# Emitting three RWKV quads ahead of the windowed attention, and spreading the residual's spill over weight chunks

## The chip, the cores and the metric

The kernel runs on one core of one Trainium2 chip. The metric is the device time of one execution in microseconds (us). TensorE (PE) does matrix products into PSUM, VectorE (DVE) and ScalarE (ACT) do element-wise work, GpSimd (POOL) a few memory fills, and SyncE (SP) starts nearly all transfers (DMA). Each engine runs its own instructions strictly in the order in which they stand in the program and waits on semaphores for the others.

## The reference

A sequence of 256 tokens of width 2048 passes through two blocks. The first (S5 and DeltaNet branches, then a gated feed-forward net) and the context path of the second are not touched. In the second block, cut to what matters here:

```python
x = rmsnorm(first_block(x), final_norm_w)                 # the residual of the second block
z = modulate(rmsnorm(x), sh1, sc1) @ w_in
q, k, v = axial_rope(...)                                 # 16 query heads, 4 key/value heads of 64
attn = windowed_gqa(q, k, v, kc, vc, sink)                # softmax over a band and 256 context tokens
r, v, kk, dirs, gate = rwkv_prepare(z)                    # 16 heads of 64, two directions
for d in range(2):                                        # S = S*w + (S.-kk) b^T + v k^T ; y = S r
    y += wkv_scan(S_ctx[d], r, w[d], k[d], v, kk, a[d], reverse=d == 1)
rw = (groupnorm(y) + bonus) * gate
x = x + g1 * (concat(attn, rw) @ w_out)
x = x + g2 * swiglu(modulate(rmsnorm(x), sh2, sc2))
return rmsnorm(x, final_norm_g)
```

## The kernel before

Activations lie feature-major (features on the 128 partitions, 256 tokens along the free axis). Every large product goes through `dense`: a weight chunk of 256 by up to 512 elements is loaded, ACT rounds it (`wr`, L269), DVE takes the remainder (`wl`, L270), and PE does three products of 256 columns for each 128x128 block (L298, L299, L301), 24 for a full chunk. The chunk has three load buffers and two for each half.

The RWKV recurrence is done by `rw_quad`, four heads at a time, in chunks of 64 tokens. A quad has a front (`rw_front`: gates, decays, the operands BK and AR, then chunk products that become the masked N and M, L1355), the inverse of a triangular matrix in 16x16 blocks on DVE (L571 to L607), a merge of the blocks to 64x64 in which PE, DVE and ACT take turns (L627 to L655), and four chunk steps, each of which needs the state S left by the one before: px (PE, L1433), X (DVE, L1436), pa (PE, L1445), two copies into SAV (ACT L1447, DVE L1448), pS (PE, L1452), two updates of S (DVE, L1458 and L1459). `rw_quad` is a generator, and `early` draws from several so that a quad's front is emitted before the one ahead of it ends.

`attention` runs over 4 key/value heads, 2 query blocks and 2 pairs of heads: 16 units. A unit is at_ps (PE, L1667 and L1670), two row maxima (DVE, L1674), their scaling (L1676, once a unit), two exponentials (ACT, L1680), transposes (PE, L1683), copies (L1685) and at_po (PE, L1689). After two units the sums are inverted and the result is scaled (L1706). `attn_split`, `x3_load` (the residual read back from memory) and `w_out2(0)`, the output projection of the attention's half in 384 products, follow; then the gate (`rw_out_gate`, L1547 to L1549), the group norm `rw_out` for the four quads (L1565 to L1578, with the root at L416, the reciprocal at L417 and the spread at L425), and `w_out2(1)`.

`x2_spill` scales the residual by the norm of the first block's end in 16 DVE instructions (L1174) and writes it out in four transfers. It is called between the projection of the first keys and `rw_lora`.

Each engine's order is made by a scheduler that takes, of what is ready in its own model of time, the instruction that was emitted first. So the order of calls in `program` is an order of priority, and work that is emitted later fills the places where earlier work can't run. All of it is fixed before the run.

Of the kernel before, what the change touches and what calls it, by code (L numbers as in the profile page):

```python
# [14 lines left out]
ALU = mybir.AluOpType  # L15
# [74 lines left out]
class Kern:  # L90
# [182 lines left out]
    def dense(self, W, KT, c0, w, xh, xl, evac, r0=0):  # L273
# [7 lines left out]
        for k0 in range(0, KT, 2):  # L281
# [7 lines left out]
            for b, part in order:  # L289
                for j in range(b * per, min(b * per + per, nft)):  # L290
                    m = min(128, w - j * 128)
                    o = banks[b][:m, j % per]
                    first_j, last_j = j % per == 0, j % per == per - 1 or j == nft - 1
                    for k in range(kb):
                        kt = k0 + k
                        a = (wr, wl)[part][:, k, j * 128:j * 128 + m]
                        if part == 0:
                            nc.tensor.matmul(o, lhsT=a, rhs=xh(kt), start=kt == 0 and first_j, stop=False)  # L298
                            nc.tensor.matmul(o, lhsT=a, rhs=xl(kt), start=False, stop=False)  # L299
                        else:  # L300
                            nc.tensor.matmul(o, lhsT=a, rhs=xh(kt), start=False, stop=kt == KT - 1 and last_j)  # L301
            self.ticks += self.tick_rate
            while self.ticks >= 1:
                self.ticks -= 1
# [2 lines left out]
        for i, b in enumerate(banks):  # L307
            evac(i, b)


    ticks = 0.0
    tick_rate = 0.72
# [851 lines left out]
    def x2_spill(self):  # L1164
        nc = self.nc
        x = self.x1
        fw = self.P("final_norm_w")
        r = self.rsqrt(self.s1, 1.0 / (32 * D), self.eps["e6"])
        self.x2d = self.pd.tile([D, T], F32, name="x2d")
        xd = self.x2d.rearrange("(k p) t -> p k t", p=128)  # L1170
        for i, t in enumerate(x.tiles):
            for k in range(4):
                kt = i * 4 + k
                nc.vector.scalar_tensor_tensor(x(kt), x(kt), fw[:, kt:kt + 1], r, ALU.mult, ALU.mult)  # L1174
            nc.sync.dma_start(xd[:, i * 4:i * 4 + 4], t)

    def mod1(self):

# [342 lines left out]
    def rw_x(self, half):  # L1521
        h = (self.hh, self.hl)
        if half == 0:

            self.rwR = {"kkn": [None, None]}
            self.rw_cols(self.rwR, h, "k", "x", 0)
            self.x2_spill()
            self.rw_lora(self.rwR, h, "x")
        self.rw_cols(self.rwR, h, "kvr"[1 - half:], "x", half)
        if half:  # L1530
# [254 lines left out]
    def program(self, out):  # L1785
# [28 lines left out]
        self.rw_x(1)  # L1814
        self.attn_cols()
        self.ada_end()
        self.attention()
        self.early([self.rw_xq(1, ()), self.rw_xq(2, ('AR',)), self.rw_xq(3, ('AR',))])
        self.attn_split()
        self.x3_load()  # L1820
        self.w_out2(0)
# [112 lines left out]
```

## Time and profile before

| what | value |
|---|---|
| median of 3 runs | 3485.99 us (3480.36 to 3486.3) |
| the profiled execution | 3484.27 us, its span 3482.5 us |
| PE busy | 3341.5 us (96%), 30680 instructions |
| DVE busy | 2506.8 us (72%), 4245 instructions |
| ACT busy | 1515.8 us (44%), 2148 instructions |
| granted TensorE clock | 0.975 of 2.4 GHz over the span |

The profiled execution lies 1.7 us under the median, so sums are made against 3484.27 us. Times in the trace are counted from the span's start. In the rows below a busy PE is not PE at its peak: products are pipelined, and at the lower clock level each takes longer and still counts as busy. Of the order's rows, fp32 products appear twice in the trace's counts.

### The profile page before, as it was taken

The numbers are of one execution on the slowest core, as the hardware profiler recorded it, in microseconds if no ns is written. First come the engines' busy times: TensorE is split into PE (matmuls) and PEld (weight loads), VectorE is DVE, ScalarE is ACT, GpSimd is POOL, SyncE is SP. The second block draws the span as 40 slices with busy tenths as digits, with TensorE's granted clock in tenths as the row PEclk, the third lists the DMA queues.
The fourth block names the chain that finished last, engine by engine and source line by source line (L and its number), as shares of the span: only waits on it lengthen the run. The fifth ranks groups of instructions, "written<-read, shape, count | busy, mean of one in ns | idle before, by whom it ended". The sixth has DMA issues, their size and how long they took to land. (4 is left out here: it accounts for less than half of the span.)

```text
span 3482.5 us, 72752 instructions
## 1 busy us (share of the span) xinstructions
PE 3341.5 (96%) x30680; PEld 3073.5 (88%) x30680; DVE 2506.8 (72%) x4245; ACT 1515.8 (44%) x2148; POOL 17.0 (0%) x46
## 2 busy tenths in 40 slices
PE   8999999999999999999999999998898999999998
PEld 7889767898998889999999988886686999999997
DVE  7787777877668878967777778686666666665556
ACT  5434334444454444434444454443433443333433
POOL 0000000000000000000000000000000000000000
PEclk9999999999998999999999999997899999999999
DMA  7655555667654445456676664450123676655554
GB/s 234 184 167 172 179 173 183 190 217 254 209 176 158 139 160 165 157 192 225 227 230 219 223 198 148 141 174 2 33 98 100 211 226 225 228 188 182 182 187 146
DMA packets 337287, 618.37 MB, mean 178 GB/s; under 512 B 25184, under 2 KB 49504, under 8 KB 336960
## 3 DMA queue, kind: packets, MB, share of 16 engines
q1 hardware_dynamic: 336736, 612.66, 54.7%
q8 instruction: 240, 3.93, 0.5%
q0 software_dynamic: 224, 1.07, 0.1%
q14 instruction: 87, 0.71, 0.1%
HBM read 608.39 MB, written 4.72 MB: 176 GB/s over the span
## 5 line engine op out<-in xcount | busy, mean ns | idle before, releaser
L270 DVE TENSOR_TENSOR wl<-w,wr 128x1024 fp32r<-128x1024 f32 (+2 forms) x928 | 1110.5, 1197 | 654.2 <-ACT wr L269 619.8
L269 ACT CAST wr<-w 128x1024 fp32r<-128x1024 f32 (+2 forms) x928 | 953.3, 1028 | 1382.6 <-PE acc L299 1172.0
L298 PE MATMUL acc<-hh,wr 128*128 128x256 f32 (+2 forms) x4976 | 1255.1, 287 | 35.0 <-DVE conv L378 10.3
L299 PE MATMUL acc<-hl,wr 128*128 128x256 f32 (+2 forms) x4976 | 1247.8, 286 | 5.1 <-DVE hl L317 3.2
L298 PEld LDWEIGHTS acc<-hh,wr 128*128 128x128 f32 (+2 forms) x4976 | 957.7, 193 | 75.5 <-issue 31.3
L299 PEld LDWEIGHTS acc<-hl,wr 128*128 128x128 f32 (+2 forms) x4976 | 958.6, 193 | 22.7 <-issue 16.4
L301 PE MATMUL acc<-hh,wl 128*128 128x256 f32 (+2 forms) x4976 | 749.6, 286 | 6.5 <-DVE wl L270 6.4
L301 PEld LDWEIGHTS acc<-hh,wl 128*128 128x128 f32 (+2 forms) x4976 | 660.5, 193 | 30.9 <-DVE wl L270 10.9
L298 PE MATMUL acc<-hid,wr 128*128 128x256 f32 x1408 | 355.6, 286 | 3.1 <-DVE x L1128 3.0
L299 PE MATMUL acc<-hid,wr 128*128 128x256 f32 x1408 | 353.3, 284 | 0.0
L298 PEld LDWEIGHTS acc<-hid,wr 128*128 128x128 f32 x1408 | 270.2, 192 | 7.2 <-DVE x L1128 3.7
L299 PEld LDWEIGHTS acc<-hid,wr 128*128 128x128 f32 x1408 | 270.3, 192 | 1.5 <-issue 1.1
L242 DVE SCALAR_TENSOR_TENSOR w_ada<-w_ada,ada_c 128x512 f32<-128x512 f32 x384 | 260.2, 679 | 3.8 <-PE ada_c L235 3.3
L301 PE MATMUL acc<-hid,wl 128*128 128x256 f32 x1408 | 223.9, 285 | 1.5 <-DVE wl L270 1.5
L301 PEld LDWEIGHTS acc<-hid,wl 128*128 128x128 f32 x1408 | 191.9, 192 | 4.4 <-DVE wl L270 1.9
L1107 DVE SCALAR_TENSOR_TENSOR fconv<-acc,pv,fconv 128x255 f32<-128x255 f32 (+1 forms) x176 | 81.2, 477 | 16.5 <-ACT fconv L1105 14.7
L298 PE MATMUL acc<-mrgh,wr 128*128 128x256 f32 x256 | 65.1, 289 | 2.9 <-ACT wr L269 2.9
L299 PE MATMUL acc<-ys5l,wr 128*128 128x256 f32 x256 | 64.3, 287 | 2.3 <-DVE ys5l L317 2.3
L298 PE MATMUL acc<-ys5h,wr 128*128 128x256 f32 x256 | 64.1, 287 | 1.1 <-ACT ys5h L316 1.0
L1352 PE MATMUL rw_ps<-rw_AR,rw_BK 64*128 64x64 f32 (+1 forms) x512 | 61.0, 294 | 4.0 <-ACT rw_BKT L1359 2.4
L299 PE MATMUL acc<-mrgl,wr 128*128 128x256 f32 x256 | 64.4, 287 | 0.0
L1105 ACT ACTIVATE fconv<-acc,pv 128x256 f32<-128x256 f32 x88 | 40.4, 471 | 53.2 <-PE acc L301 27.7
(537 smaller groups left out, 3733.2 us busy)
## 6 DMA issues: line engine op xcount, KB each, us to landing
w<-in_w_dram SPq DMA_DIRECT2D x264, 512.0 KB, 3.6
w<-in_w_in_dram SPq DMA_DIRECT2D x256, 512.0 KB, 4.0
w_ada<-in_ada_wT_dram SPq DMA_DIRECT2D x384, 256.0 KB, 4.2
w<-in_ffn_up_dram SPq DMA_DIRECT2D x176, 512.0 KB, 4.1
w<-in_ffn_down_dram SPq DMA_DIRECT2D x88, 512.0 KB, 4.1
w<-in_w_out_dram SPq DMA_DIRECT2D x64, 512.0 KB, 4.3
w_ada<-in_ada_w_dram SPq DMA_DIRECT2D x64, 256.0 KB, 2.7
w<-in_glu_w_dram SPq DMA_DIRECT2D x32, 512.0 KB, 4.2
```

The source lines that it names most:

```text
L242: nc.vector.scalar_tensor_tensor(w, w, 1.0, ps, ALU.mult, ALU.mult, accum_out=self.part[:, n - n0, q:q + 1])
L269: nc.scalar.copy(r[:, :kb, :w], t[:, :kb, :w])
L270: self.wsub = nc.vector.tensor_tensor(l[:, :kb, :w], t[:, :kb, :w], r[:, :kb, :w].bitcast(F32), ALU.subtract)
L298: nc.tensor.matmul(o, lhsT=a, rhs=xh(kt), start=kt == 0 and first_j, stop=False)
L299: nc.tensor.matmul(o, lhsT=a, rhs=xl(kt), start=False, stop=False)
L301: nc.tensor.matmul(o, lhsT=a, rhs=xh(kt), start=False, stop=kt == KT - 1 and last_j)
L1105: nc.scalar.activation(t[:, j], ps[:, j], AF.Copy, scale=w(2))
L1107: v.scalar_tensor_tensor(t[:, j, k:], ps[:, j, :256 - k], w(2 - k), t[:, j, k:], ALU.mult, ALU.add)
L1352: nc.tensor.matmul(pss[e][:, c], lhsT=bk(d, c)[hs[e]], rhs=AR[hs[e], d, :, cs], start=True, stop=True)
```

## The change

`program` now calls `early` with quads 1 to 3 before `attention`, not after it. `x2_spill` is now a generator that `dense` draws from once a chunk; each of its 16 instructions is queued on DVE behind the newest `wl`.

```diff
@@ dense
+            next(self.beside, None)
             self.ticks += self.tick_rate
...
+    beside = iter(())
@@ x2_spill
             for k in range(4):
                 kt = i * 4 + k
-                nc.vector.scalar_tensor_tensor(x(kt), x(kt), fw[:, kt:kt + 1], r, ALU.mult, ALU.mult)
-            nc.sync.dma_start(xd[:, i * 4:i * 4 + 4], t)
+                with self.tc.issue_after(self.wsub.ins):
+                    nc.vector.scalar_tensor_tensor(x(kt), x(kt), fw[:, kt:kt + 1], r, ALU.mult, ALU.mult)
+                if k == 3:
+                    nc.sync.dma_start(xd[:, i * 4:i * 4 + 4], t)
+                yield
@@ rw_x
-            self.x2_spill()
+
+            self.beside = self.x2_spill()
             self.rw_lora(self.rwR, h, "x")
@@ program
         self.ada_end()
+
+        self.early([self.rw_xq(1, ()), self.rw_xq(2, ('AR',)), self.rw_xq(3, ('AR',))])
         self.attention()
-        self.early([self.rw_xq(1, ()), self.rw_xq(2, ('AR',)), self.rw_xq(3, ('AR',))])
         self.attn_split()
```

The order on PE just behind the last projection (`attn_cols`) was, before the change, as follows: inv is the merge of quad 1, at_ps and at_pt are the attention's first unit.

```order
L627 MATMUL inv_27714<-invD,rw_N_27344 32x32 x2
L1667 MATMUL at_ps<-at_ks,at_qs 128x512 x2
L1670 LDWEIGHTS at_mi
L1670 MATMUL at_ps<-at_mi 128x128
...
L1683 MATMUL at_pt<-cst,at_p 128x128 x4
L635 MATMUL inv_27781<-invDT,invB_27779 32x16 x23
```

With the change (lines from 302 on are shifted by 2 to 6) the same place on PE reads so; these are the merge's end, chunk steps of quad 1 and the front of quad 2, and the first at_ps stands behind the next quad's merge.

```order
L1438 MATMUL rw_px<-rw_S,rw_AR 64x64 x8
L1446 MATMUL rw_py<-rw_AR,rw_S 64x64 x8
L652 MATMUL inv_27143<-invDT,invBT 32x32 x31
L1450 MATMUL rw_pa<-rw_X,invDT_26970 64x64 x8
L1457 MATMUL rw_pS<-rw_SAV_26812,rw_BKT 64x64
...
L1357 MATMUL rw_ps<-rw_AR,rw_BK 128x128 x8
L1467 MATMUL rw_py<-rw_M_26690,rw_SAV_26813 64x64 x4
...
L637 MATMUL inv_27729<-invDT,invB_27727 32x16 x64
L1673 MATMUL at_ps<-at_ks,at_qs 128x512 x2
L1676 LDWEIGHTS at_mi
```

All of quad 1, the front and the inverse of quad 2 and the front of quad 3 moved ahead of the attention's first product; from the last at_pv to the first at_ps, 544 of the quads' products follow each other.

At the attention's end PE had, before, the front of quad 3 (rw_ps, rw_pt) and the first products of w_out2(0) (acc from ath) in turns.

```order
L1462 MATMUL rw_py<-rw_M_28162,rw_SAV_28243 64x64 x4
L1358 MATMUL rw_pt<-cst,rw_BK 128x128 x4
L1352 MATMUL rw_ps<-rw_AR,rw_BK 128x128 x8
L298 MATMUL acc_29421<-ath_29405,wr 128x256
L299 MATMUL acc_29421<-atl_29407,wr 128x256
...
L1352 MATMUL rw_ps<-rw_AR,rw_BK 128x128 x4
```

With the change no quad is left there: the attention's last unit is followed by w_out2(0) alone, and the 16 gate products and the group norms of quads 1 to 3 (rw_mean, ns, rw_rs) stand behind it.

```order
L1695 MATMUL at_po<-at_PT,vt 64x128
L1704 MATMUL at_rt<-cst,ts_c_28665 4x128
L298 MATMUL acc_29421<-ath_29405,wr 128x256
L299 MATMUL acc_29421<-atl_29407,wr 128x256
...
L1553 MATMUL rw_pg<-rw_g,g_up_29925 128x256
L1554 MATMUL rw_pg<-rw_g,g_up_29926 128x256
L1571 MATMUL rw_mean<-xr_23824,cst 128x256
L408 MATMUL ns<-sq,cst 32x256
...
L427 MATMUL rw_rs<-rw_nsq,cst 128x256 x2
```

So quad 3 left the stretch of w_out2(0) for that of the attention, and three of the four group norms stand bare behind the dense products.

On DVE the spill stood in one block before (x_0 to x_3, with one reciprocal inside):

```order
L1174 SCALAR_TENSOR_TENSOR x_0_8690<-x_0_8690,pv,rs 128x256 x4
L1174 SCALAR_TENSOR_TENSOR x_1_8691<-x_1_8691,pv,rs 128x256 x4
L1174 SCALAR_TENSOR_TENSOR x_2_8692<-x_2_8692,pv,rs 128x256 x4
L1174 SCALAR_TENSOR_TENSOR x_3_8693<-x_3_8693,pv,rs 128x256 x2
L417 RECIPROCAL rw_nsq<-rw_nsq 128x256
L1174 SCALAR_TENSOR_TENSOR x_3_8693<-x_3_8693,pv,rs 128x256 x2
L270 TENSOR_TENSOR wl<-w,wr 128x1024 x2
```

With the change it reads so there:

```order
L1177 SCALAR_TENSOR_TENSOR x_0_8690<-x_0_8690,pv,rs 128x256 x4
L1177 SCALAR_TENSOR_TENSOR x_1_8691<-x_1_8691,pv,rs 128x256 x4
L270 TENSOR_TENSOR wl<-w,wr 128x1024
L1177 SCALAR_TENSOR_TENSOR x_2_8692<-x_2_8692,pv,rs 128x256
L242 SCALAR_TENSOR_TENSOR w_ada,part<-w_ada,ada_c 128x512
L419 RECIPROCAL rw_nsq<-rw_nsq 128x256
L270 TENSOR_TENSOR wl<-w,wr 128x1024
```

Eight of the 16 still form a block, the other eight stand one behind each of the next `wl`, and the reciprocal has moved behind the first `wl`.

## Rows read from the trace of the kernel before

**Rows 1.** Stretches: length; PE, PEld, DVE, ACT, POOL busy (count); clock; DMA share; GB/s.
```profile
2337.50:2358.00 20.50, 7.52 (x150) 3.83 (x148) 19.13 (x36) 14.33 (x32) 0.00 (x0) 0.74 0.26 74
2358.00:2389.60 31.60, 29.15 (x408) 21.78 (x410) 18.92 (x44) 10.83 (x25) 1.04 (x2) 0.57 0.01 2
2415.00:2445.00 30.00, 24.66 (x167) 18.08 (x166) 24.87 (x60) 10.62 (x25) 1.04 (x2) 0.89 0.01 2
2358.00:2524.90 166.90, 147.45 (x1957) 108.71 (x1958) 105.10 (x253) 65.32 (x166) 3.13 (x9) 0.81 0.06 18
2524.90:2636.90 112.00, 103.33 (x1295) 83.75 (x1293) 70.75 (x129) 41.45 (x69) 0.87 (x2) 0.94 0.23 77
2800.00:2900.00 100.00, 100.00 (x836) 100.00 (x835) 64.50 (x89) 38.82 (x41) 0.00 (x0) 1.00 0.72 228
```
**Rows 2.** DVE's timeline: first scaled maximum, last scaling of the attention (start, duration).
```profile
2358.01 0.15 DVE L1676 SCALAR_TENSOR_TENSOR s_mag<-s_mag,at_nsk 128x2 f32<-128x2 f32 x1
...
2524.49 0.42 DVE L1706 TENSOR_TENSOR qT<-at_po,at_rc 128x256 f32<-128x256 f32 x1 [0.90 <-ACT at_rc L1705]
```
**Rows 3.** PE's timeline: first product of w_out2(1).
```profile
2636.93 0.58 PE L298 MATMUL acc<-rwh,wr 128*128 128x256 f32 x1
```
**Rows 4.** DVE by line, 2338 to 2640: count, busy us, mean ns, idle before.
```profile
L571 DVE STREAM_TRANSPOSE invL<-rw_N 32x512 f32<-32x512 f32 x8 | 8.5, 1063 | 0.1
L1355 DVE TENSOR_TENSOR rw_N<-rw_ps,cst 128x256 f32<-128x256 f32 x16 | 6.7, 421 | 6.2 <-PE rw_ps L1352 6.1
L1326 DVE SCALAR_TENSOR_TENSOR rw_BK<-rw_cum,rw_ta 64x512 f32<-64x512 f32 x8 | 5.5, 683 | 0.1
L1448 DVE COPY rw_SAV<-rw_pa 64x256 f32<-64x256 f32 x12 | 5.1, 428 | 14.0 <-ACT rw_SAV L1447 13.9
```
**Rows 5.** PE's timeline: a chunk step's products at either clock level.
```profile
2378.78 1.12 PE L1433 MATMUL rw_px<-rw_S,rw_AR 64*64 64x64 f32 x16
...
2383.56 1.69 PE L1445 MATMUL rw_pa<-rw_X,invDT 64*64 64x64 f32 x16
...
2391.37 0.68 PE L1433 MATMUL rw_px<-rw_S,rw_AR 64*64 64x64 f32 x16
```
**Rows 6.** DVE's timeline: two units beside chunk steps; a merge from L637 to L1459.
```profile
2397.64 0.16 DVE L1676 SCALAR_TENSOR_TENSOR s_mag<-s_mag,at_nsk 128x2 f32<-128x2 f32 x1
...
2404.79 0.16 DVE L1676 SCALAR_TENSOR_TENSOR s_mag<-s_mag,at_nsk 128x2 f32<-128x2 f32 x1
...
2481.95 0.48 DVE L637 SCALAR_TENSOR_TENSOR invDT<-inv,cst,invDT 128x256 f32<-128x256 f32 x1
...
2502.24 0.42 DVE L1459 TENSOR_TENSOR rw_S<-rw_S,rw_el 128x256 f32<-128x256 f32 x1
```
**Rows 7.** PE's timeline: the last of 16 pairs of gate products.
```profile
2606.30 0.69 PE L1548 MATMUL rw_pg<-rw_g,g_up 32*128 32x256 f32 x2
```
**Rows 8.** Chain of waits (start, us, what): a group norm with nothing beside it.
```profile
2629.16 1.15 PE rw_mean L1565 x2
...
2633.98 1.75 DVE rw_nsq L417
2635.78 1.22 PE rw_rs L425 x4
```
**Rows 9.** ACT's timeline around the table load.
```profile
2612.22 1.28 ACT L416 ACT_TABLE_LOAD   x1
2613.52 0.47 ACT L416 ACTIVATE rw_nsq<-ns,eps_lnx 64x256 f32<-64x256 f32 x1
```
**Rows 10.** DVE's timeline at the spill.
```profile
2051.12 5.62 DVE L1174 SCALAR_TENSOR_TENSOR x<-x,pv,rs 128x256 f32<-128x256 f32 x14
2056.66 1.75 DVE L417 RECIPROCAL rw_nsq<-rw_nsq 128x256 f32<-128x256 f32 x1
```
**Rows 11.** Stretches at the spill, columns as in rows 1.
```profile
2055.00:2060.00 5.00, 1.47 (x5) 0.55 (x3) 5.00 (x9) 0.47 (x1) 0.00 (x0) 0.72 0.88 312
2060.00:2065.00 5.00, 4.71 (x25) 4.71 (x26) 4.92 (x10) 1.89 (x2) 0.00 (x0) 0.59 0.96 290
```

## The prediction, made before the changed kernel had run

> **What bounds the kernel now.** I read the windows first, then the DVE timeline for where stages begin and end, then the groups by line, then the chain of waits. Over most of the span dense products fill PE: 836 of them in 100 us, 0.12 us each, at the upper clock level (1.00, 2.4 GHz), with DVE at 64% [rows 1]. The edit works where this doesn't hold. Four marks cut that place up. The last projection ends near 2337.5; the attention's first scaled maximum is at 2358.0 and its last scaling at 2524.5 to 2524.9 [rows 2]; the first product of w_out2(1) starts at 2636.9 [rows 3]. So before the change: a lead-in of 20.5 us, 166.9 us of attention with quad 1's merge and chunks, quad 2 and quad 3's operands beside it, and a tail of 112.0 us with w_out2(0), the rest of quad 3, the gate and the group norms [rows 1]. In the lead-in DVE is busy 19.1 of 20.5 us with 36 instructions. In the attention no engine is full: DVE 105 of 167 us, and PE counts 147 at a clock of 0.81, so many of its products ran at the lower level (1.2 GHz). In the tail PE is busy 103 of 112 us: there quad 3's turns between the engines are covered by dense products.
>
> **The spill (first part).** DVE runs 14 scalings in 5.62 us and the 1.75 us reciprocal back to back before the next wl [rows 10]; PE is busy 1.47 of the 5 us from 2055 and runs 25 products at clock 0.59 in the next 5 [rows 11], where 42 fit by 0.12 us. The stall costs 3.5 us of idling and about 17 x 0.12 = 2.0 us of lost pace. In the new order wl stands behind 8 scalings, not 16, and ahead of the reciprocal: it comes 8 x 0.4 + 1.75 = 5 us earlier, enough for most of the stall. The other eight scalings stand behind later wl's, in chunks of 24 x 0.12 = 2.9 us of PE, where DVE has a wl of 1.2 and less than one more instruction: hidden. Two of the four spill transfers move behind chunk loads on SP; their reader, x3_load, comes hundreds of us later. I take -4.5 us, between -7 and 0 (the stall only moves).
>
> **The lead-in (quad work before the first unit).** This is the term that decides. DVE's list from the last projection to the first L1676 grows from 36 to 167 instructions; counted by line, 133 come and two copies of queries go. Those that come: 16 masks at 0.42, 6 transposes at about 1.07, 12 BK products and 4 scans at 0.68 (24 us), and 95 others at about 0.42 (39 us, by L1448's size) [rows 4]. Less the two copies this is 62 us of durations; neighbours overlap a little (36 instructions of the lead-in sum to 20.4 us by line and take 19.1 of busy time), so 58 us. DVE is in order and the first maximum stands behind all of it.
>
> That is a floor, since a bare quad also waits. A chunk step is px, X, pa, two SAV copies, pS, two S updates, one after the other. At 2.4 GHz px took 0.68, at the lower level 1.12, and pa 1.69 [rows 5]; the five element-wise steps take about 0.4 each [rows 4]. With pS like px and 0.1 us for each of eight hand-overs (an estimate; the reciprocal to its product takes 0.05 in rows 8), a step takes 0.68 x 3 + 2.1 + 0.8 = 4.9 us at the upper and 1.12 x 2 + 1.69 + 2.9 = 6.8 us at the lower level, of which DVE works 1.7. So 3 to 5 us of waiting in each of three steps, 2.5 in the last; about 5 in quad 1's merge, where DVE has BK of the next pair to do; 5 in quad 2's masks, which wait for rw_ps (6.2 us idle before 16 of them, [rows 4]); 5 in the inverse, quad 3's front and the first unit. I take 28 us, between 10 (all filled by other DVE work) and 40 (lower clock throughout). The lead-in becomes longer by 58 + 28 = 86 us (68 to 98). Before the change, the same work hid in attention and dense products.
>
> **The attention.** It keeps its 16 units; beside them now lie quad 2's merge and chunks, all of quad 3 from the masks on, and one group norm. By the order DVE has 193 instructions here, before 250. Pieces, by the nearest rows: five units beside chunk steps at 7.7 (7.15 between two maxima at 2397.6 and 2404.8 [rows 6], up to 8 elsewhere), 38.5 us; the merge of quad 2 with two units, which begins ahead of the first maximum, 11, and that of quad 3 with two, 21 (20.3 from L637 to L1459 [rows 6]); four units with masks and inverse, 40 (the like stretch has DVE busy 24.9 of 30 us [rows 1], and their DVE work is 36 us of durations); the last three units, nearly bare, with one root and two table loads, 27. Sum 138, against 166.9: -29 us, between -42 (bare units at 5 us, merges overlapped) and -17.
>
> Two table loads are new in that piece (the root of the group norm among exponentials), 1.28 us each; the root starts 0.02 us behind the load [rows 9], so 2.6 us. The Trainium skill, ScalarE: Activation LUTs, section "What ACT_TABLE_LOAD costs", gives 1283 ns and a drain of about 1380 ns beside it, which would make 5.3 us, an estimate by that page. The trace agrees on the load and shows no drain in front of or behind it; the sum goes by the trace.
>
> **The tail.** w_out2(0) has 384 products; 22 stand ahead of the attention's last scaling, 362 x 0.12 = 43.4 us remain, and 2 us for a start at the lower level. The loads lead by five chunks, and the chunk queued behind x3_load on SP is needed 14 us later, so no wait there. Then 15 of 16 rows of gate products at 0.63 us (the last pair took 0.69 with overlap [rows 7]), 9.4 us, and three group norms in series, each from mean to spread 2629.2 to 2636.4 = 7.1 us [rows 8], with one table load: 22.6. Together 77.4 against 112.0: -35 us, between -44 (norms at 6, gate faster) and -27 (norms at 9). What covered quad 3 is gone from here, and so is quad 3; what is late next is the group norm, with nothing beside it.
>
> **Sum.** -4.5 + 86 - 29 - 35 = +17.5; 3484.3 + 17.5 = 3502 us. What lies behind w_out2(1) is the same in both. Against the median it is +16.
>
> **Rivals.** *Faster: the chains pack.* If DVE finds other work in nearly every hand-over, the lead-in costs 70, the attention saves 40, the tail 43 and the spill 6: -19, 3465 us. For it: DVE had only 195 of the 299 us from 2337.5 to 2636.9, so there is room. Against: in the one stretch of rows where a merge runs, 20.3 us hold 9.6 us of DVE work even with attention beside it. It decides from the point where the lead-in's waits fall under 10 us and bare units under 6. Chance 0.13.
>
> *No change.* Waits of 18 us in the lead-in (76), -35 in the attention, -37 in the tail, -4.5: 0, 3484 us. For it: each of the three is inside its own bounds, and sums by hand of waits tend to count some twice. Chance 0.17.
>
> *The lower clock holds all through the lead-in.* In the lead-in and the next 31.6 us the clock is 0.74 and 0.57 though attention fills PE there [rows 1]; without it the steps above take 6.8 us, rw_ps too doubles its pace, and the waits reach 40: +98 in place of 86, 3514 us, and with w_out2(0) starting low 3516. Chance 0.2, inside slower. The Trainium skill, TensorE: Matmul & The Clock Gate, Part 1, says that the throttled state is the default and that activity releases it; by that the bare quad would run low, as the trace's 0.57 suggests.
>
> The likeliest, +8 to +26 us, has 0.5. Chances: faster by over 0.2% (7 us, about what a measurement of this kernel can tell from none) 0.13; within it 0.17; slower 0.7. The range that holds the time 8 times in 10 goes from 3474, most of the way to the faster case, to 3522, past the low-clock case; the likeliest one's own range is 3492 to 3510.
>
> **What would show it.** In the new profile, the first L1676 should come near 2358 - 4.5 + 86 = 2440, with PE under half busy before it; the attention's last scaling near 2578 and the first product of w_out2(1) near 2655. Dense products of w_out2(0) should run without a hole, and ahead of w_out2(1) some 20 us should show PE waiting for L417 and L1568. At the spill PE should be busy nearly throughout 2050 to 2060. I am wrong in the lead-in if the first L1676 comes before 2425, in the attention if it takes under 125 us or over 150, in the tail if it takes under 68 or over 85.

## The result and the profile after

The change makes the kernel slower: 3522.35 us (median of 4 runs, 3519.66 to 3523.48) against 3486.14 us; the ratio is 1.0103, 95% interval 1.0089 to 1.0117, so +36 us (+31 to +41). The forecast was 3502 with a range to 3522, so the time lies just past the range's end. The sign was right, the size was short by half.

The profiled run took 3523.48 us (span 3521.6, before 3482.5: +39.1). The windows of the changed kernel, columns as in [rows 1], for lead-in, attention, tail, and then two pieces of the tail (the dense products, and the bare group norms, those with nothing beside them):

```profile
2336.10:2438.90 102.80, 56.50 (x1147) 43.77 (x1148) 75.04 (x167) 36.30 (x82) 2.52 (x6) 0.68 0.06 16
2438.90:2592.10 153.20, 139.13 (x1837) 105.34 (x1833) 83.35 (x195) 60.15 (x152) 1.48 (x4) 0.85 0.05 16
2592.10:2676.26 84.16, 68.85 (x433) 53.24 (x431) 41.80 (x60) 27.05 (x37) 0.00 (x0) 0.84 0.31 108
2592.10:2636.40 44.30, 44.05 (x366) 43.70 (x364) 25.17 (x30) 16.90 (x17) 0.00 (x0) 1.00 0.53 182
2645.80:2676.26 30.46, 15.40 (x38) 5.12 (x37) 14.62 (x27) 7.68 (x17) 0.00 (x0) 0.57 0.00 0
```

The marks that bound them answer to [rows 2, 3]: the first scaled maximum and the last scaling on DVE,

```profile
2438.91 0.15 DVE L1682 SCALAR_TENSOR_TENSOR s_mag<-s_mag,at_nsk 128x2 f32<-128x2 f32 x1
...
2591.57 0.42 DVE L1712 TENSOR_TENSOR qT<-at_po,at_rc 128x256 f32<-128x256 f32 x1 [5.49 <-ACT at_rc L1711]
```

and on PE the first product of w_out2(1):

```profile
2676.26 0.58 PE L298 MATMUL acc<-rwh,wr 128*128 128x256 f32 x1
```

From these rows, against the forecast (us):

| piece | before | after | change | forecast |
|---|---|---|---|---|
| up to the last projection, with the spill | 2337.5 | 2336.1 | -1.4 | -4.5 |
| lead-in | 20.5 | 102.8 | +82.3 | +86 |
| attention | 166.9 | 153.2 | -13.7 | -29 |
| tail | 112.0 | 84.2 | -27.8 | -35 |
| sum | | | +39.4 | +17.5 |

The first scaled maximum stands at 2438.9 where 2440 was forecast: the cost came out almost as forecast. What was overrated is what comes back. Of the 21.9 us between 39.4 and 17.5, the attention holds 15.3, the tail 7.2, the spill 3.1, and the lead-in takes 3.7 off. The three norms that stand bare are, by the program's order, those of quads 0 to 2 (the section on the change has 1 to 3): it is quad 3's norm that moved into the attention.

At the spill the row that answers to [rows 11] has PE busy 4.69 of 5 us at clock 1.00, before 1.47 at 0.72:

```profile
2055.00:2060.00 5.00, 4.69 (x37) 4.35 (x36) 5.00 (x8) 1.72 (x3) 0.00 (x0) 1.00 1.04 344
2060.00:2065.00 5.00, 5.00 (x40) 4.61 (x40) 5.00 (x10) 1.05 (x1) 0.00 (x0) 1.00 0.86 267
```

### The profile page after: what moved, and what is told of

Same layout as the page of the kernel before. It is cut to its first block, busy times and chain, and to the rows that moved or that the text cites. A ratio compares the mean times of both kernels' runs of the same rounds, so it can differ in the third digit from the quotient of the medians.

```text
span 3521.6 us, 72772 instructions
## 1 busy us (share of the span) xinstructions
PE 3349.9 (95%) x30680; PEld 3082.0 (88%) x30680; DVE 2508.0 (71%) x4245; ACT 1516.3 (43%) x2150; POOL 17.0 (0%) x46
## 4 chain that ended last, share of the span: by engine, by line
PE 87%; DVE 9%; ACT 2%; issue 1%; DMA 1%; ACTq 0%; DVEq 0%; SPq 0%; POOLq 0%
PE acc L298 24%; PE acc L299 24%; PE acc L301 24%; DVE wl L270 1%; PE rw_ps L1357 1%; PE ada_ps L201 1%; PE s_py L962 1%; PE s_pw L942 1%; PE at_pt L1689 1%; ACT wr L269 1%; PE rw_pS L1457 1%; PE ss L332 1%; PE at_ps L1673 1%; PE ns L408 1%; PE at_po L1695 1%
## 5 line engine op out<-in xcount | busy, mean ns | idle before, releaser
L299 PEld LDWEIGHTS acc<-hl,wr 128*128 128x128 f32 (+2 forms) x4976 | 959.9, 193 | 23.8 <-issue 17.8
```

## The experiments

In the table each run's trace is cut by the same five marks: the 13,801st dense product, the last dense product of the projections, the first scaled maximum, the end of the last scaling, and the first product of w_out2(1). The lead-in is counted here from the start of the last dense product, 4.7 us earlier than above. What follows the last mark takes 843 to 846 us in all runs but the ninth (854.1). Runs with a ratio have 4 to 12 executions beside those of the kernel before; runs with a time in us have one. The kernel before, measured beside each, had medians of 3483.6 to 3489.2. Single profiled runs differ: the first column spreads over 8 us among runs with the changed spill and an unchanged quad 0, and the attention takes 166.9 and 160.5 us in two runs with the old order of calls (before, 1), 153.1 and 148.0 in two with the new one (after, 2). Differences of less than about 6 us in one stretch of one run are not read.

| run | time, or ratio to before | up to | projections | lead-in | attention | tail |
|---|---|---|---|---|---|---|
| before | 3486.14 | 2174.1 | 158.6 | 25.2 | 166.9 | 112.0 |
| after | 1.0103 | 2173.0 | 158.4 | 107.5 | 153.1 | 84.3 |
| 1 spill alone | 0.9985 | 2175.8 | 158.0 | 26.6 | 160.5 | 114.0 |
| 2 quads alone | 1.0119 | 2179.7 | 158.2 | 107.6 | 148.0 | 86.7 |
| 3 after, small maxima | 3522.39 | 2171.9 | 158.4 | 106.8 | 153.9 | 84.3 |
| 4 after, no state in y | 3518.87 | 2176.1 | 156.3 | 107.8 | 146.1 | 85.2 |
| 5 after, other norm buffers | 3529.62 | 2177.4 | 158.0 | 106.3 | 167.7 | 73.6 |
| 6 quads in the projections | 1.0205 | 2179.9 | 298.9 | 50.7 | 102.9 | 85.2 |
| 7 the same, norms in the attention | 1.0167 | 2175.2 | 297.7 | 52.2 | 118.7 | 60.9 |
| 8 spill alone, norms beside quad 3 | 0.9992 | 2177.8 | 158.2 | 26.6 | 161.8 | 116.3 |
| 9 before, small maxima | 3472.46 | 2172.6 | 158.2 | 24.4 | 152.5 | 108.8 |
| 10 after, v early in all quads | 1.0088 | 2187.4 | 162.4 | 90.9 | 151.7 | 84.3 |
| 11 six steps in the projections | 1.0056 | 2173.7 | 187.8 | 17.6 | 171.0 | 109.5 |
| 12 eight steps, v early | 1.0030 | 2181.7 | 181.8 | 19.2 | 156.7 | 108.4 |
| 13 before, no state in y | 3488.52 | 2181.0 | 157.0 | 26.6 | 172.7 | 104.0 |
| 14 after, both cuts | 3524.14 | 2176.6 | 156.0 | 115.7 | 145.2 | 84.3 |
| 15 after, v early in quads 1 to 3 | 1.0052 | 2172.0 | 165.7 | 88.9 | 145.8 | 83.7 |
| 16 spill alone, v early in quads 1 to 3 | 0.9961 | 2177.5 | 165.5 | 18.0 | 160.2 | 109.5 |

### 1 and 2: each part alone

Run 1 is the changed kernel with the order of calls of before:

```diff
-        self.early([self.rw_xq(1, ()), self.rw_xq(2, ('AR',)), self.rw_xq(3, ('AR',))])
         self.attention()
+        self.early([self.rw_xq(1, ()), self.rw_xq(2, ('AR',)), self.rw_xq(3, ('AR',))])
```

> The spill runs beside the chunks, and the quads stay behind the attention as before. Theory: the spill frees PE by about 4.7 us at 2050 to 2065 (in the changed kernel PE was 4.75 us ahead of before at 2067 by the same dense product), and part of that is lost again before 2180, where the changed kernel was 1.2 us ahead: 3481 to 3485 us, ratio 0.9985 to 0.9997. Rival: the loss before 2180 came from the moved quads, and all 4.7 us stay: 3481.4 or less, ratio 0.9987 or less. Second rival: nothing is left of it, 1.000.

Run 2 has the new order and the spill in one block again (`self.run(self.x2_spill())`, without `issue_after`).

> Only the quads are emitted ahead of the attention; the spill is one block as before. Theory: the two parts add, and this part costs +40 us: first scaled maximum about 82 us later behind the last projection than before, attention 14 us shorter, tail 28 us shorter; 3523 to 3528 us, ratio 1.0105 to 1.012. Rival: the quads' position and the spill work on each other (other places of the same instructions on DVE), then it is off by more than 4 us from that.

Measured: 0.9985 (0.9973 to 0.9997) and 1.0119 (1.0104 to 1.0133). Their product is 1.0104, the change itself 1.0103: the parts add, and they act on each other by nothing that shows. The spill gives -5 us (-9 to -1), the quads cost +41. In the changed kernel's trace the 13,201st dense product starts 4.4 us earlier than before and the 13,801st 1.1 earlier, but that holds what the two runs had gained or lost long before. Taken from the 13,101st, just ahead of the stall, the traces agree better: to the 13,201st the four with the spill in one block take 18.9 to 19.7 us, the twelve with it beside the chunks and v unmoved in quad 0 take 13.4 to 14.1; from there to the 13,801st it is 101.9 to 103.7 against 103.6 to 108.2. So the stall gives 5 to 6 us, 2 to 3 go back in what follows, and about 3 remain, in run 1 (119.4 in all) as in the changed kernel (119.2). The moved quads don't cause the loss: of run 1's expectation the theory holds in this, though its time and ratio lie at the rival's.

### 3, 4, 9, 13 and 14: what sets the attention

Two cuts, each in the kernel before and in the changed one, and in the changed one both together. The first takes each row maximum over 128 of the 512 keys, which shrinks DVE's work; the second leaves out the products that read the state into y, so that y is incomplete, and shrinks PE's:

```diff
-                        v.tensor_reduce(mx[:, i + e:i + e + 1], ps[e], AX.X, ALU.max)
+                        v.tensor_reduce(mx[:, i + e:i + e + 1], ps[e][:, 256:384], AX.X, ALU.max)
```

```diff
-                for p, d, e in pde:
-                    nc.tensor.matmul(py[hs[e], p, d], lhsT=S[hs[e], p, d], rhs=ARs[p][hs[e], d, 1, cs],
-                                     start=p == d == 0, stop=False)
...
-... rhs=Ms[p][:, e, d, c], start=False,
+... rhs=Ms[p][:, e, d, c], start=p == d == 0,
```

> The changed kernel, but each row maximum of the attention is taken over 128 of the 512 keys, so that 32 DVE instructions of 0.68 us become about 0.2 us: 15 us of DVE leave the attention's stretch, and nothing on PE changes. Theory (the attention is set by PE's own products and by the turns between PE, ACT and DVE): from the first scaled maximum to the last scaling 153 us become 145 to 150. Rival (it is set by DVE's work, as the prediction counted it): 153 becomes 140 or less, and the time 3508 or less.

> The changed kernel without the eight products per chunk that read the state into y (the second half of y's sum alone remains): in the attention's stretch 128 products with 6.4 us of PE go, in the lead-in 64 with 3.5 us; DVE keeps every instruction. Theory (PE is the bound beside chunk steps): the attention becomes 5 to 8 us shorter, the lead-in by 0 to 2. Rival (DVE sets the attention): 0 to 2 us in the attention.

> The kernel before, with each row maximum taken over 128 of the 512 keys (32 DVE instructions of 0.68 us become about 0.2 us), as in the third experiment. Theory (PE and the turns set the attention in both kernels, so that its DVE count was the wrong count to size it by): the attention's 167 us stay within 160 to 170. Rival (DVE, which has 105 us of work there against 83 after the change, was the bound before the change and only stopped being it): 155 or less.

> The kernel before without the eight products per chunk that read the state into y (as in the fourth experiment). About 150 of them lie in the attention. Theory (DVE and the turns bound the attention before the change, PE after it): the attention's 160 to 167 us become 0 to 3 us shorter. Rival (PE is a bound in both kernels): 6 us or more shorter.

> The changed kernel with maxima over 128 of 512 keys and without the products that read the state into y. Alone the first cut gave +0.8 us in the attention and the second -7.0. Theory (PE is the bound there): together -6 to -9, 144 to 147 us. Rival (with less PE work DVE becomes the bound at once, so that the first cut counts beside the second): 140 or less.

The attention's window in each, columns as above (DVE is the third busy time, PE the first). First the changed kernel with small maxima, without the state in y, and with both cuts:

```profile
2437.02:2590.88 153.86, 138.50 (x1835) 104.66 (x1831) 72.40 (x195) 59.92 (x152) 1.48 (x4) 0.83 0.05 15
```

```profile
2440.22:2586.30 146.08, 129.00 (x1703) 95.41 (x1699) 83.48 (x195) 60.39 (x152) 1.48 (x4) 0.89 0.05 16
```

```profile
2448.22:2593.41 145.19, 130.93 (x1707) 97.36 (x1703) 72.55 (x195) 60.03 (x152) 1.48 (x4) 0.87 0.05 16
```

Then the kernel before with small maxima, and without the state in y:

```profile
2355.30:2507.79 152.49, 134.50 (x1889) 100.70 (x1889) 90.37 (x243) 63.74 (x165) 2.97 (x8) 0.85 0.06 20
```

```profile
2364.53:2537.22 172.69, 150.18 (x1886) 109.60 (x1886) 107.03 (x259) 66.80 (x169) 4.00 (x10) 0.81 0.05 18
```

And without either cut, run 1 (the old order), run 2 and run 15 (the new one):

```profile
2360.40:2520.90 160.50, 142.67 (x1958) 105.56 (x1958) 104.01 (x249) 65.13 (x166) 3.18 (x9) 0.83 0.06 19
```

```profile
2445.50:2593.47 147.97, 134.18 (x1831) 101.03 (x1827) 83.07 (x195) 60.86 (x152) 1.49 (x4) 0.89 0.05 16
```

```profile
2426.60:2572.40 145.80, 131.88 (x1835) 99.22 (x1830) 83.81 (x195) 60.80 (x152) 1.49 (x4) 0.91 0.05 16
```

From these rows, with PE's idle time as length less busy time:

| run | length | PE busy | PE idle | clock | products | DVE busy |
|---|---|---|---|---|---|---|
| before | 166.9 | 147.5 | 19.5 | 0.81 | 1957 | 105.1 |
| 1 | 160.5 | 142.7 | 17.8 | 0.83 | 1958 | 104.0 |
| 9, DVE's cut | 152.5 | 134.5 | 18.0 | 0.85 | 1889 | 90.4 |
| 13, PE's cut | 172.7 | 150.2 | 22.5 | 0.81 | 1886 | 107.0 |
| after | 153.2 | 139.1 | 14.1 | 0.85 | 1837 | 83.4 |
| 2 | 148.0 | 134.2 | 13.8 | 0.89 | 1831 | 83.1 |
| 15 | 145.8 | 131.9 | 13.9 | 0.91 | 1835 | 83.8 |
| 3, DVE's cut | 153.9 | 138.5 | 15.4 | 0.83 | 1835 | 72.4 |
| 4, PE's cut | 146.1 | 129.0 | 17.1 | 0.89 | 1703 | 83.5 |
| 14, both | 145.2 | 130.9 | 14.3 | 0.87 | 1707 | 72.6 |

After, 2 and 15 have nearly the same products and PE idles 14 us in each; what differs is PE's busy time, and it goes with the granted clock of the stretch. That is most of the 5 to 8 us by which traces of like orders differ.

DVE's cut takes 11 us from its busy time in the changed kernel, and the stretch doesn't get shorter (153.9, outside the 145 to 150 expected). So after the change DVE's work there costs nothing that shows. PE's cut gave -7.0 us against the changed kernel, as expected, but only -1.9 against run 2, which had the same granted clock (0.89): beside run 2, PE's busy time falls by 5.2 us and its idle time grows by 3.3. So PE's products alone don't set the stretch either, as far as one execution shows.

In the kernel before, PE's cut takes nothing from the stretch. DVE's cut goes with a stretch that is 8 to 14 us shorter (152.5 against 160.5 and 166.9), and run 9 missed its expectation, which had said that DVE would not count before either. But it doesn't show the rival, that DVE was the bound: PE idles 18.0 us, as in run 1. What fell is PE's busy time, with 68 products fewer in the stretch and 64 more in the tail, since shorter maxima made the scheduler choose another order. Attention and tail together hold as many products as in run 1 (3248 for 3253) and are 13 us shorter with PE idle as long (26.4 us for 25.4); the granted clock is higher in both. Whether that comes from DVE's work, from the order, or from this one execution stays open.

The changed kernel's waits in that stretch agree with run 3 (who waits, for what: us in total, times, longest). DVE's largest:

```profile
DVE s_mag L1680 <- PE at_ps L1676: 19.7, 19, 2.8
DVE at_PT L1691 <- PE at_pt L1689: 11.7, 8, 7.7
```

and PE's:

```profile
PE at_pt L1689 <- ACT at_p L1686: 8.1, 7, 2.7
PE at_po L1695 <- issue: 3.2, 1, 3.2
PE rw_pb L1412 <- DVE rw_M L1360: 1.0, 1, 1.0
```

DVE waits mostly for PE's scores and transposes, PE for ACT's exponentials, and PE for DVE hardly at all.

### 5, 7 and 8: the group norms

In the changed kernel the three bare norms take 30.4 us. Their spreads on PE are 11 us apart:

```profile
2653.27 1.23 PE L427 MATMUL rw_rs<-rw_nsq,cst 32*128 32x256 f32 x4 [2.60 <-DVE rw_nsq L419]
...
2664.26 1.22 PE L427 MATMUL rw_rs<-rw_nsq,cst 32*128 32x256 f32 x4 [2.34 <-DVE rw_nsq L419]
...
2675.10 1.22 PE L427 MATMUL rw_rs<-rw_nsq,cst 32*128 32x256 f32 x4 [2.34 <-DVE rw_nsq L419]
```

Before the change the spreads of the same norms were already 9.0 and 11.0 us apart:

```profile
2615.82 0.70 PE L425 MATMUL rw_rs<-rw_nsq,cst 32*128 32x256 f32 x4 [1.95 <-DVE rw_nsq L417]
...
2624.80 0.70 PE L425 MATMUL rw_rs<-rw_nsq,cst 32*128 32x256 f32 x4 [1.56 <-DVE rw_nsq L417]
...
2635.78 0.80 PE L425 MATMUL rw_rs<-rw_nsq,cst 32*128 32x256 f32 x2 [0.41 <-DVE rw_nsq L417]
```

A norm takes its tiles from two pools, that is, rings of buffers: `pacc` and `te` for quads 0 to 2, `pm` and `t1` for quad 3. Run 5 gives neighbouring norms different pools:

```diff
-        ps_ = (lambda name: self.pacc(name=name)[:, 0]) if hq < 3 else lambda name: self.pm([128, 256], name=name)
-        sb = self.te if hq < 3 else self.t1
+        ps_ = (lambda name: self.pacc(name=name)[:, 0]) if hq % 2 == 0 else lambda name: self.pm([128, 256], name=name)
+        sb = self.te if hq % 2 == 0 else self.t1
```

> The changed kernel, but the group norms of quads 1 and 3 take their PSUM and SBUF tiles from the other pools, so that neighbours no longer share a ring of buffers. In the changed kernel the three bare norms lie 11 us apart and take 30.4 us from the first mean to w_out2(1). Theory (each norm waits for the buffers of the one before it): 30.4 becomes 18 to 24 us, and the time 3510 to 3517. Rival (they are in series because PE, ACT and DVE run in order and at the lower clock level): it stays above 28 us and the time above 3519.

The tail lost 10.7 us, 84.3 to 73.6, because one more norm now stands in the attention, which was 14.6 us longer, at a granted clock of 0.79 where it had 0.85. The two norms left stand 10.4 us apart (spreads at 2671.47 and 2681.86). That reads like the rival, but it is no test of the theory: by the program's order the norms that moved are those of quads 1 and 3, both on the other pools now, and the two left are those of quads 0 and 2, which share their pools as before. Neighbours on different pools stand in other traces. Before the change the norm behind the three above is quad 3's; its means run between those of quad 2, and its spread follows 5.2 us behind:

```profile
2625.43 1.13 PE L1565 MATMUL rw_mean<-xr,cst 128*128 128x256 f32 x4
...
2641.02 0.70 PE L425 MATMUL rw_rs<-rw_nsq,cst 32*128 32x256 f32 x4
```

The same pair is 5.4 us apart in run 1, and in runs 11, 12 and 16 two norms on different pools follow each other within 2.3 to 4.5 us, while neighbours on the same pools are 9.0 to 11.0 us apart in the rows above. (In runs 9 and 13 most of the last norm runs beside `w_out2(1)`, so that its distance says nothing.) So the traces speak for the buffers, or for the order that the scheduler makes by them. No run has three bare norms with neighbours on different pools, and what spaces them stays open.

Runs 7 and 8 move all norms. Run 7 is run 6 (below) with gate and norms emitted before `w_out2(0)` and all norms on `pm` and `t1`, the pools that the quads use; run 8 is run 1 with the gate and the norms of quads 0 to 2 emitted before `w_out2(0)`.

```diff
-        self.w_out2(0)
         self.rw_out_gate()
-        for hq in range(4):
+        for hq in range(3):
             self.rw_out(hq)
+        self.w_out2(0)
+        self.rw_out(3)
```

> As the one with the quads in the projection, and the gate and the group norms take their tiles from the pools that the quads use and are emitted before w_out2(0), so that most of the norms stand in the attention and none behind w_out2(0). Theory: another 20 to 28 us less than that kernel, 3430 to 3470. Rival (the norms hold up the attention, whose PE was the bound): 5 us or less.

> The kernel before with the spill beside the chunks, and with the gate and the norms of quads 0 to 2 emitted before w_out2(0). By the order these norms then stand among quad 3's turns, the norm of quad 3 among the dense products, and none behind them. Theory (a bare norm costs 9 to 11 us on PE's chain, one in a quad's turns nothing): tail 114 us becomes 95 to 105, time 3464 to 3474. Rival (the norms push the dense products out of quad 3's turns, so that what is hidden there costs as much again): 3474 to 3484.

In run 7 the tail is 24.3 us shorter than in run 6 and the attention 15.8 longer: two thirds of a bare norm's price are paid again in the attention. By the ratios it is 13 us under run 6, between the theory's 20 to 28 and the rival's 5; the times expected were far off because run 6's were. In run 8 (0.9992, 0.9983 to 1.0001) the tail is 116.3 us against 114.0 in run 1, so nothing is gained; the time, 3483.72, lies in the rival's range. That the dense products then need behind the norms what the norms took of quad 3's turns fits it, but isn't shown apart.

### 6, 11 and 12: dense products as cover

Run 6 calls `early` before `attn_cols`, so that the projections' dense products are there to fill quads' turns.

```diff
+        self.early([self.rw_xq(1, ()), self.rw_xq(2, ('AR',)), self.rw_xq(3, ('AR',))])
         self.attn_cols()
         self.ada_end()
-        self.early([self.rw_xq(1, ()), self.rw_xq(2, ('AR',)), self.rw_xq(3, ('AR',))])
         self.attention()
```

> The changed kernel with the call of early ahead of attn_cols, so that the quads' turns have the dense products of the attention's projections beside them; nothing else. Theory (the 82 us of lead-in are work and turns without cover, not work that PE has no room for): between the last projection and the first scaled maximum 25 us or less remain, the projections become 40 to 70 us longer, the attention 110 to 130, the tail as in the changed kernel, 84; 3455 to 3490 us. Rival (PE is full in the projections, so that the quads cost there what they cost bare): 3515 or more.

1.0205 (1.0191 to 1.0219): slower still. Of the lead-in 50.7 us are left where 25 or less were expected. The attention, nearly without quads, falls to 102.9 us, 6.4 per unit, but the projections grow by 140. PE is not full there; in the middle of them it stands:

```profile
2260.00:2340.00 80.00, 50.46 (x760) 42.79 (x761) 63.78 (x136) 24.50 (x50) 1.48 (x4) 0.72 0.24 72
```

Its largest waits between 2180 and 2479 are

```profile
PE rw_pv L1403 <- ACT rw_vr L1397: 24.5, 2, 14.3
PE inv L637 <- ACT invB L632: 12.4, 2, 6.2
PE inv L644 <- DVE invD L640: 5.2, 2, 4.6
```

The time is the rival's, by another cause than it named: weights for the next dense products were ready, but in PE's fixed order these products stood behind others that were not. The next chunk's `wl` is written from 2289.36 on, in the middle of the first wait at rw_pv (2286.0 to 2300.3), and the first dense product behind it starts 110 us later, 1198 products on in PE's order:

```profile
2289.36 1.23 DVE L270 TENSOR_TENSOR wl<-w,wr 128x1024 fp32r<-128x1024 f32 x1
```

```profile
2399.47 1.20 PE L298 MATMUL acc<-hh,wr 128*128 128x256 f32 x1
```

What is emitted first is placed first where the scheduler's model of time has it ready; that its model has these waits shorter than the chip is a supposition, no run was made on it.

Runs 11 and 12 draw only the first six or eight of the quads' steps, one behind each chunk of the projections (`self.beside = itertools.islice(steps, 6)`), and leave the rest behind the attention; run 12 has the early copy of v of run 10 too.

> Quads 1 to 3 behind the attention as before, but the first six of their steps (quad 1, and the front of quad 2) drawn one behind each weight chunk of the projections; by the order 342 of their products stand among the projections' last 690 dense ones, 64 in the lead-in, 617 in the attention and 305 in the tail (before: 82, 92, 720, 434). Theory (PE's own products cost 0.05 to 0.1 us each wherever PE is the bound, and the gain is in turns that dense products cover): projection +15 to +30 us, attention -10 to -20, tail -15 to -25: 3455 to 3480 us. Rival (as with all quads in the projections, PE stands at products that are not ready while dense ones wait behind them): projection +40 or more and 3485 or above.

> As the one before, with eight steps and with v's copy and transposes ahead of the inverse. By the order 358, 42, 689 and 231 of the quads' products in the four stretches. Theory (the wait at rw_pv is what made the projections dear): 3450 to 3475, and 5 us or more below the one with six steps. Rival (another wait takes its place): within 3 us of that one or above it.

1.0056 (1.0043 to 1.0068) and 1.0030 (1.0020 to 1.0041). Both are slower than before. In run 11 the projections grow by 29 us, as expected, and the lead-in shrinks by 8, but neither attention nor tail gives anything back (171.0 and 109.5 us); the time is the rival's. Run 12 is 11 us under it, as its theory said, though not at the time that it gave.

### 10, 15 and 16: a wait that is order alone

In the lead-in of the changed kernel PE's largest waits (total, times, longest) are

```profile
PE inv L644 <- DVE invD L640: 11.5, 2, 6.9
PE inv L637 <- ACT invB L632: 10.8, 2, 6.0
PE rw_pv L1403 <- ACT rw_vr L1397: 10.6, 1, 10.6
PE at_ps L1673 <- DVE at_qs L1660: 5.8, 1, 5.8
```

The third is a plain reversed copy of v, ready long before. ACT's timeline shows why it is late: it stands behind the inverse's last activations (L606), which wait 12.1 us for DVE.

```profile
2399.81 0.72 ACT L606 ACTIVATE invL<-invR,cst 128x256 f32<-128x256 f32 x1 [12.13 <-DVE invR L602]
2400.44 0.49 ACT L606 ACTIVATE invtmp<-invR,cst 128x256 f32<-128x256 f32 x1
2400.84 0.60 ACT L1397 COPY rw_vr<-xv 128x512 f32<-128x512 f32 x1
```

Behind rw_pv on PE stand the first products of quad 3's front, which don't need the inverse. Run 10 emits the inverse after v's copy, transposes and their copies:

```diff
-        dT, dN = self.inv(lambda h: Nu[h][hs[h]])
         SAV = [al("SAV")([128, 2, 2, 2, 2, 64], name=f"rw_SAV{i}") for i in range(2)]
...
+        dT, dN = self.inv(lambda h: Nu[h][hs[h]])
         if out:
```

> The changed kernel, with v's reversed copy, its eight transposes and their copies emitted ahead of the inverse of each quad, not behind it. In the changed kernel PE stands 10.6 us at rw_pv in the lead-in, because that copy waits on ACT behind the inverse's last two activations, and behind rw_pv stand the first products of quad 3's front. Theory (this wait in order is a part of the lead-in's 28 us of waits): the lead-in becomes 5 to 10 us shorter and the time 3512 to 3518. Rival (DVE is busy with the inverse meanwhile and sets the lead-in): 0 to 2 us, 3520 or more.

Run 15 does that for quads 1 to 3 alone, and run 16 does it with the quads behind the attention (run 1 and this).

> The changed kernel with v's copy, transposes and their copies ahead of the inverse for quads 1 to 3 only. With it for all quads the lead-in with the projections became 12.6 us shorter, but the products up to the first of the projections came 14 us later. Theory (the 10.6 us at rw_pv are a wait of order alone; the loss came from quad 0): 3507 to 3513 us. Rival (what goes in the lead-in comes back in the attention): 3518 or more.

> The spill beside the chunks, the quads behind the attention as before, and v's copy and transposes ahead of the inverse for quads 1 to 3. Theory (in that order PE has attention and dense products beside the wait, so that nothing is gained by it): the same as the spill alone within 4 us, 3474 to 3482. Rival (the wait holds quad 3 back in the tail): 3462 to 3473.

Run 10 took 16.6 us off the lead-in and lost 14 ahead of the first mark. Run 15's expectation puts that loss on quad 0, but the edit reaches the four quads of the context path too, and the loss is there: from the 5,001st dense product to the 13,101st, ahead of quad 0, runs 10 and 12 (which has the same edit) take 1194.7 and 1191.7 us, all others 1180.9 to 1187.8; from there to the 13,801st they take 119.9 and 120.1, no more than the others (117.1 to 123.4). So run 12's time holds about 9 us that its eight steps didn't cost. Run 15 keeps the gain without the loss: 1.0052 (1.0034 to 1.0069), 3505.61 us, half of what the change had cost and a little better than its theory. In its lead-in rw_pv no longer stands in the list of waits; the first three are

```profile
PE inv L644 <- DVE invD L640: 8.3, 2, 7.0
PE inv L637 <- ACT invB L632: 6.6, 2, 5.7
PE at_ps L1679 <- DVE at_qs L1666: 5.8, 1, 5.8
```

Lead-in and projections together are 11.3 us shorter than after the change. The attention is 7.3 shorter, but against run 2 only 2.2; its granted clock was the highest (0.91).

Run 16 is the fastest of the versions that keep all the work: 0.9961 (0.9947 to 0.9976), -14 us (-18 to -8) against the kernel before. Its theory had expected no more than the spill alone. Its time, 3474.23, lies just inside the theory's range, but by the ratios, each against the kernel before beside it, it is 8 us better than run 1, the two intervals overlapping by a hair. In its trace the tail is 4.5 us shorter than in run 1 (109.5 for 114.0), where the rival puts the gain, and little differs elsewhere; 4.5 us in one stretch of one run is no more than traces differ by, so where the gain lies isn't shown:

```profile
2343.00:2361.10 18.10, 6.88 (x125) 3.83 (x123) 11.31 (x17) 9.71 (x21) 0.00 (x0) 0.71 0.40 115
2361.10:2521.20 160.10, 142.43 (x2008) 105.91 (x2010) 107.18 (x256) 67.12 (x172) 4.01 (x10) 0.87 0.06 19
2521.20:2630.80 109.60, 99.89 (x1253) 78.81 (x1249) 70.88 (x125) 40.35 (x68) 0.00 (x0) 0.90 0.24 78
```

The lead-in is 8.6 us shorter too, but the projections are 7.5 longer, where that work went.

## Why the prediction was wrong, step by step

**The spill.** Right in mechanism, and nearly in size. PE runs through 2055 to 2065 at the upper level (2.4 GHz, clock 1.00). Run 1 as a whole gave -5 us (-9 to -1) for -4.5; counted on the spot, 5 to 6 us come back and about 3 remain.

**The lead-in.** The sum was right, and in part by luck. DVE is busy 75.0 us against 19.1, +55.9 for the 58 worked out (its durations add up to 63, where 62 stands), and idle 27.8 us against 1.4, +26.4 for the 28 chosen. Of its idle time the chunk steps take 11 us, where 11.5 to 17.5 were counted, and quad 2's masks 2.4 for 5. Quad 3's front takes 7.8 us in two waits, where 5 were counted for it, the inverse and the first unit together; the products of PE that they wait for stand behind rw_pv, whose wait was not foreseen (see 10, 15 and 16 above). The longer one is

```profile
2411.57 0.43 DVE L1312 TENSOR_SCALAR rw_th<-rw_th 128x512 f32<-128x512 f32 x1 [5.20 <-ACT rw_th L1310]
```

A bare chunk step, between 4.9 and 6.8 us by the prediction, shows between two X's on DVE; the last three steps begin 5.1 and 4.6 us apart (the first two 8.9, with the merge's end between them):

```profile
2367.32 0.42 DVE L1441 TENSOR_TENSOR rw_X<-rw_px,rw_P 128x256 f32<-128x256 f32 x1 [1.30 <-PE rw_px L1438]
2372.38 0.42 DVE L1441 TENSOR_TENSOR rw_X<-rw_px,rw_P 128x256 f32<-128x256 f32 x1 [0.86 <-PE rw_px L1438]
2376.93 0.42 DVE L1441 TENSOR_TENSOR rw_X<-rw_px,rw_P 128x256 f32<-128x256 f32 x1 [0.47 <-PE rw_px L1438]
```

So these steps ran near the pace of the upper level, and the rival of a lower clock throughout falls here, though the mean is 0.68, so that PE was at the lower level for more than half of the lead-in. In run 14, with the same work on DVE there, the mean was 0.59, and the lead-in took 8 us longer (115.7 for 107.5). Not seen was that 10.6 us of PE's waits are no chain of the recurrence but the order on ACT; runs 10 and 15 showed it.

**The attention: the step that failed.** "By the order DVE has 193 instructions here, before 250", and the pieces made of them summed to 138 us; measured are 153.2, over the 150 that the prediction named as its sign of being wrong. The sentence under it was "In the attention no engine is full: DVE 105 of 167 us, and PE counts 147". PE was the fuller one, and the move takes little from it: quad 2's chunks and quad 3 come in where quad 1's and quad 2's front leave, 1957 products before and 1837 after. By that count PE's 147.45 us [rows 1] become 138.4; measured are 139.1, so close in part by luck, since PE's busy time for these products is 132 to 139 us by the granted clock. A stretch of 138 us would have needed PE almost without a hole, where it had 19.5 us of them before and has 14.1 now. The check needed one division by numbers that lay in the first row read. The 13.7 us that came back are 8.3 us of PE's busy time and 5.4 of its idle time. The changed kernel and runs 2, 3 and 15 take 145.8 to 153.9 us there, run 1 and the kernel before 160.5 and 166.9, so 7 to 21 us come back, never 29. By pieces, the two merges with two units each were the error: each held one, 13.4 and 20.8 us between two maxima, the first of them from 2438.91 above:

```profile
2452.29 0.16 DVE L1682 SCALAR_TENSOR_TENSOR s_mag<-s_mag,at_nsk 128x2 f32<-128x2 f32 x1
...
2510.78 0.16 DVE L1682 SCALAR_TENSOR_TENSOR s_mag<-s_mag,at_nsk 128x2 f32<-128x2 f32 x1
2531.55 0.16 DVE L1682 SCALAR_TENSOR_TENSOR s_mag<-s_mag,at_nsk 128x2 f32<-128x2 f32 x1
```

Run 3 shows that DVE's work is covered there after the change. Whether it was before, run 9 leaves open.

**The tail.** Dense products and gate came out as worked out (44.3 us to the gate for 45.4, 9.4 for 9.4); the 2 us for a start at the lower level didn't come, the clock was 1.00. The term of the three norms, 22.6 us, measured 30.4. Its 7.1 us were read from a pair of norms that ran interleaved: quad 2's first mean had run at 2625.43, 3.7 us ahead of the mean in [rows 8], and quad 3's steps lay between its own; to the end of its spread, 2637.0, even these rows give 7.8. The distance of two spreads of norms in series, 9.0 to 11.0 us before the change, was the row to take. Why those that share their pools stand in series, and the pair before didn't, is in the section on the norms, as far as it is known.

**Table loads.** The attention has the two new loads. Of the first, ACT's timeline shows 1.28 us and the root right behind it:

```profile
2570.78 1.28 ACT L418 ACT_TABLE_LOAD   x1
2572.07 0.47 ACT L418 ACTIVATE rw_nsq<-ns,eps_lnx 64x256 f32<-64x256 f32 x1
```

The drain that the Trainium skill (ScalarE: Activation LUTs, section "What ACT_TABLE_LOAD costs") puts beside a load doesn't show here either; the sum by the trace was the right one.

**The chances.** The case that came true, slower, had 0.7. The range had its top at the price of a lower clock in the lead-in, and no rival in which the attention gives back half: the bound of -17 for it was the nearest, and -13.7 lies outside. The tail, -27.8, came near its bound of -27.

What stays open: what makes up the 14 us in which PE idles in the attention after the change (its own cut gave between -1.9 and -7.0), why the granted clock of that stretch differs between traces of like orders (0.83 to 0.91), whether DVE's work set its length before, and what spaces the bare norms.

## What to carry to other kernels

Size a stretch by every engine that the move touches: scale each engine's busy time by the work that leaves and comes, and let no forecast go below the largest. Read the price of a step that repeats from the distance between two of its ends, not from the length of one. Before a cut of one engine's work is read as its price, see that the scheduled order stayed the same, and compare busy time, idle time and clock apart. Work emitted early in a fixed order can cost twice, once bare and once by what it holds up: look for cheap instructions that stand behind a long wait on an engine that runs in order, and emit those first.

## What the runs showed that was not expected

PE idles 3.2 us in the attention of the changed kernel with no releaser ("issue" in the waits above), from 2514.2 to 2517.4, 4 us behind the issue of two of the residual's loads at 2509.9. The like shows at the same product in runs 3 (3.1 us) and 5 (2.9 us), as long behind the same loads, and not in runs 2, 4, 14 and 15, though the loads are there too. What PE waits for there its semaphores don't say. The records of the instruction queue q8 show that a block of 16 KB is fetched within each of the three holes: it starts 0.4 to 0.6 us behind the hole's beginning and lands 1.4 to 1.5 us ahead of its end (2514.83 to 2515.93 in the changed kernel), and the block before it came 16 to 20 us earlier. That PE waits for its own instructions fits this; no run was made on it.
